# A hybrid encoder's second layer: the first attention units' buffers move, and two tiles' first key pairs come first

## The chip, the cores and the metric

The kernel runs on one core of a Trainium2 chip. The metric is the device time of one execution in microseconds (us): 3005.96 us is the median of three runs of the kernel before (3002.47, 3012.47, 3005.96). The engines are TensorE (PE; its weight loads are listed as PEld), VectorE (DVE), ScalarE (ACT), GpSimd (POOL) and SyncE (SP), which here only issues transfers.

## The reference

A two-layer encoder over 2048 tokens of width 1024, all in float32. Layer 0 (a state-space scan and a convolution branch) is not touched by the change. Layer 1 projects the normed input to q, z, k, v and to a small indexer; the indexer scores every admissible key, each query keeps its best 256 keys, and attends to these alone with 16 heads of 64 over 4 key/value heads:

```python
isc = jax.nn.relu(jnp.einsum("bqhd,bsd->bqhs", qib, ki))
score = jnp.einsum("bqh,bqhs->bqs", wib, isc)
score = jnp.where((key_chunk <= c)[None, None, :], score, -jnp.inf)
_, idx = lax.top_k(score, ksel)
...
logits = jnp.einsum("bqhgd,bqkhd->bqhgk", qb, kg) * scale
logits = jnp.where(valid[:, :, None, None, :], logits, -jnp.inf)
ob = jnp.einsum("bqhgk,bqkhd->bqhgd", softmax(logits), vg)
return (out * jax.nn.silu(z)) @ w_out      # then residual and a final RMSNorm
```

## The kernel before

Layer 1 has three stages, in `layer1` and `layer1_out`.

*Index and projections.* The 2048 rows go through in two halves of 1024 (`project_half`). A half's normed features lie in SBUF as eight blocks, hb0 to hb7, of 8 KB a partition, each split in a high and a low part; a product of two float32 matrices is three matmuls (`mm3`: high by high, high by low, low by high). The normed input comes through four buffers xt1 of 4 KB. Each group of 256 output columns has its weights loaded (wst), split (wh on ACT, wl on POOL) and multiplied; q, z, k, v and the indexer's parts go to DRAM. `index_scores` computes the indexer's scores; `select_mask` finds the 256th best by a binary search over sort keys made of the scores' bits (key, khi, klo on DVE and ACT; a step is a count, on DVE or as a Sign on ACT, and two steps on the small tile sv, on POOL or DVE) and writes a mask to DRAM. Tiles 0 to 11 of 16 (128 queries each) are done before the last projections. Tiles 12 to 15 are done by `late`, a generator whose next step is taken beside the projections (140 steps) and then beside the attention (every 800 columns): it loads a tile's scores (scr) from DRAM (sc_d) and runs `select_mask`.

*Attention.* A unit is a query tile i and a pair of key heads kp, two half-units (hp) each; the order of tiles is the table ORDER (3, 7, 4, 6, ...), and of a tile first kp 0, then kp 1. The keys lie in SBUF, high and low part, with the values, in four sets: kh00, kl00, v00 for keys 0 to 1023 and pair 0, kh01.. for pair 1, kh10.. and kh11.. for keys 1024 to 2047. A k part is 1024 KB, a v 512 KB. `Attend.load` brings a unit's mask (amb), queries (qt) and gate (zt_a); `stacks` splits the queries on POOL into tmq, transposes them on PE (ps_q), copies them on ACT (qs); `weights` multiplies with the keys (ps_s), adds the mask and takes the minimum on DVE (lm, mx, line 1099), and takes the exp on ACT (line 1110); `values` transposes (ps_pt), copies (pT), multiplies with the values (ps_pv, line 1133), transposes back (ps_ot) and gates (zr, avt, zt_a).

*Output.* `layer1_out` loads the output weights in two halves of columns (wst3), splits them into a high part (ACT, line 1334) and a low part (POOL, some on DVE), and then takes 16 tiles: transposes (ps_t), products (ps_o), norm, store. In the code wo00 and wo10 are the high and the low part of the first half, wo01 and wo11 of the second.

What sets the order: the code is run once by a tile framework, which builds a list of instructions with their dependences and then schedules each engine's queue by its own estimate of times; a tile's memory is waited for as a whole (`reuse_waits="tile"`). Memory comes from pools stacked from the left or the right end of a partition; a pool opened where an earlier one was closed lies on the same bytes, and its first write waits for the earlier tiles' last reads. All loads and stores go through SP's one queue.

## Time and profile before

| | |
|---|---|
| median of three runs | 3005.96 us (3002.47 to 3012.47) |
| the profiled execution | 3008.15 us, its span 3006.3 us |
| granted clock of TensorE, mean over the span | 0.969 |
| PE busy | 2754.0 us, 92% of the span |
| DVE, ACT, POOL busy | 2127.9, 1694.8, 1118.3 us |
| layer 1 begins / last product of the projections / attention ends | about 960 / 1804.7 / 2809 us |
| chain that ended last, by engine | PE 41%, DVE 19%, issue 6%, ACT 5%, POOL 5%, DMA 3% |

All times are of one profiled execution and counted from the beginning of its span. A granted clock of 1.00 is 2.4 GHz, 0.50 is 1.2 GHz. Where a row names what an engine waited for, it is the one that came last by the profile's semaphore events.

### The profile page before, as it was taken

The numbers are of one execution on the slowest core, as the hardware profiler recorded it, in microseconds if no ns is written. First come the engines' busy times: TensorE is split into PE (matmuls) and PEld (weight loads), VectorE is DVE, ScalarE is ACT, GpSimd is POOL, SyncE is SP. The second block draws the span as 40 slices with busy tenths as digits, with TensorE's granted clock in tenths as the row PEclk, the third lists the DMA queues.
The fourth block names the chain that finished last, engine by engine and source line by source line (L and its number), as shares of the span: only waits on it lengthen the run. The fifth ranks groups of instructions, "written<-read, shape, count | busy, mean of one in ns | idle before, by whom it ended". The sixth has DMA issues, their size and how long they took to land.

```text
span 3006.3 us, 47629 instructions
## 1 busy us (share of the span) xinstructions
PE 2754.0 (92%) x17488; PEld 2223.8 (74%) x17488; DVE 2127.9 (71%) x4121; ACT 1694.8 (56%) x3202; POOL 1118.3 (37%) x1453
## 2 busy tenths in 40 slices
PE   7779998799999999899789898999989999999998
PEld 5657786677999898888778885666655666666787
DVE  8889895996354478979997877876777444456444
ACT  4122333334243688778856558888887767655311
POOL 3946132642231587765665323322322101001000
PEclk9889899899999999999899998999999999999999
DMA  3263554356557323223432424110110101001332
GB/s 135 72 131 127 161 158 81 114 168 194 183 186 249 100 71 109 77 84 104 140 109 77 128 92 162 38 57 29 61 38 28 49 18 43 22 5 50 123 126 98
DMA packets 233385, 300.40 MB, mean 100 GB/s; under 512 B 14144, under 2 KB 171072, under 8 KB 233024
## 3 DMA queue, kind: packets, MB, share of 16 engines
q1 hardware_dynamic: 233152, 297.37, 31.5%
q8 instruction: 137, 2.24, 0.3%
q14 instruction: 96, 0.79, 0.1%
HBM read 194.16 MB, written 105.25 MB: 100 GB/s over the span
## 4 chain that ended last, share of the span: by engine, by line
PE 41%; DVE 19%; issue 6%; ACT 5%; POOL 5%; DMA 3%; SPq 0%; DVEq 0%; ACTq 0%; POOLq 0%
PE ps_pv L1133 9%; PE ps_pt L1126 8%; PE ps_s L1095 7%; DVE eq L976 6%; PE ps_tm L121 2%; PE ps_tm L122 2%; PE ps_tm L123 2%; PE ps_o L122 2%; PE ps_o L121 2%; PE ps_o L123 2%; DVE scl L72 2%; POOL sv L69 2%; ACT eq L986 1%; DVE cum L1026 1%; POOL wl L114 1%
## 5 line engine op out<-in xcount | busy, mean ns | idle before, releaser
L114 POOL TENSOR_TENSOR wl<-wst,wh 128x512 fp32r<-128x512 f32 (+1 forms) x220 | 339.0, 1544 | 389.6 <-ACT wh L113 377.8
L121 PE MATMUL ps_tm<-wh,hb 128*128 128x256 f32 (+1 forms) x1536 | 439.4, 290 | 11.7 <-ACT ot L875 7.5
L122 PE MATMUL ps_tm<-wh,hb 128*128 128x256 f32 (+1 forms) x1536 | 444.1, 290 | 0.2 <-DVE hb L72 0.2
L123 PE MATMUL ps_tm<-wl,hb 128*128 128x256 f32 (+1 forms) x1536 | 438.8, 289 | 0.0
L1099 DVE CUSTOM_DVE_ANT_0 lm<-ps_s,amb 128x1024 f32<-128x1024 f32 (+7 forms) x256 | 250.3, 987 | 200.1 <-PE ps_pt L1126 117.2
L72 DVE SCALAR_TENSOR_TENSOR cvo<-hc,vec,cvo 128x1024 f32<-128x1024 f32 x240 | 359.3, 1529 | 0.8
L1131 ACT COPY pT<-ps_pt 128x512 f32<-128x512 f32 (+1 forms) x512 | 273.9, 564 | 152.3 <-PE ps_pt L1126 130.1
L1133 PE MATMUL ps_pv<-pT,v 128*64 128x256 f32 x2176 | 339.3, 398 | 14.4 <-DVE avt L62 7.5
L1126 PEld LDWEIGHTS ps_pt<-ident,lm 128*128 128x128 f32 x2176 | 240.1, 141 | 145.4 <-issue 124.5
L1126 PE MATMUL ps_pt<-ident,lm 128*128 128x128 f32 x2176 | 339.1, 282 | 6.1 <-ACT pT L1131 4.0
L1110 ACT ACTIVATE lm<-lm,mx 128x512 f32<-128x512 f32 (+15 forms) x256 | 309.1, 1211 | 62.9 <-DVE mx L1099 62.4
L69 POOL TENSOR_SCALAR sv<-sv 128x1 f32<-128x1 f32 x448 | 185.5, 415 | 382.6 <-DVE eq L976 296.5
L121 PEld LDWEIGHTS ps_tm<-wh,hb 128*128 128x128 f32 x1536 | 296.2, 194 | 21.2 <-ACT ot L875 9.2
L122 PEld LDWEIGHTS ps_tm<-wh,hb 128*128 128x128 f32 x1536 | 297.7, 194 | 6.0 <-DVE hb L72 0.6
L123 PEld LDWEIGHTS ps_tm<-wl,hb 128*128 128x128 f32 x1536 | 296.4, 194 | 4.8
L113 ACT CAST wh<-wst 128x512 fp32r<-128x512 f32 (+1 forms) x220 | 133.4, 610 | 277.2 <-DMA wst<-in_w_in 122.3
L1095 PE MATMUL ps_s<-kh,qs 128*128 128x512 f32 (+2 forms) x640 | 264.9, 415 | 19.4 <-DVE mx L1099 17.9
L121 PE MATMUL ps_p<-hh,wh 128*128 128x512 f32 x640 | 258.5, 406 | 19.1 <-ACT uT L520 16.0
L123 PE MATMUL ps_p<-hl,wh 128*128 128x512 f32 x640 | 258.9, 407 | 0.0
L122 PE MATMUL ps_p<-hh,wl 128*128 128x512 f32 x640 | 257.5, 403 | 0.0
L1095 PE MATMUL ps_s<-kl,qs 128*128 128x512 f32 (+2 forms) x640 | 233.4, 370 | 0.0
L913 ACT ACTIVATE relu<-ps_i 128x512 f32<-128x512 f32 (+3 forms) x304 | 161.0, 545 | 104.5 <-DVE scl L72 55.3
(327 smaller groups left out, 6353.0 us busy)
## 6 DMA issues: line engine op xcount, KB each, us to landing
wst<-in_w_in SPq DMA_DIRECT2D x168, 256.0 KB, 2.9
zs_d<-zt SPq DMA_DIRECT2D x16, 512.0 KB, 3.5
zt<-zs_d SPq DMA_DIRECT2D x16, 512.0 KB, 4.5
ry<-rec_d SPq DMA_DIRECT2D x16, 512.0 KB, 4.2
xr<-in_x SPq DMA_DIRECT2D x16, 512.0 KB, 4.3
wst<-in_w_out SPq DMA_DIRECT2D x32, 256.0 KB, 3.3
h_d<-xr SPq DMA_DIRECT2D x16, 512.0 KB, 3.5
xt<-h_d SPq DMA_DIRECT2D x16, 512.0 KB, 6.1
```

The lines of the kernel that those rows point to most:

```text
L69: eng.tensor_scalar(out=out, in0=a, scalar1=s1, scalar2=s2, op0=op0, op1=op1)
L72: self.nc.vector.scalar_tensor_tensor(out=out, in0=a, scalar=s, in1=b, op0=op0, op1=op1)
L114: nc.gpsimd.tensor_tensor(out=lo, in0=st, in1=hi.bitcast(F32), op=ALU.subtract)
L121: t.matmul(ps, a[0], b[0], start=start, stop=False)
L122: t.matmul(ps, a[1], b[0], start=False, stop=False)
L123: t.matmul(ps, a[0], b[1], start=False, stop=stop)
L1095: nc.tensor.matmul(pss[e][:, cols], qs[e][:, 2 * hp + h], src[:, e, cols], start=part == 0, stop=part == 1)
L1099: self.pace[0] = nc.vector.tensor_tensor_reduce(out=prob[e][h][:, c:c + w], in0=pss[e][:, 0:w], in1=mb[:, c:c + w], scale=-0.125, scalar=( ...
L1110: nc.scalar.activation(lm, lm, AF.Exp, bias=mxs[e, h][:, nh - 1:nh], scale=-1.0, accum_out=t["den"][:, hd:hd + 1])
L1126: nc.tensor.transpose(ps[:, s, h], prob[e][h][:, (b + s) * P:(b + s + 1) * P], ident)
L1131: nc.scalar.copy(pT[:, 0:n], ps[:, 0:n].rearrange("p s h q -> p s (h q)"))
L1133: nc.tensor.matmul(po[64 * s:64 * s + 64, e], self.kvt[(b + s) // 8, kp][2][:, (b + s) % 8, e * 64:e * 64 + 64], pT[:, s], start=b == 0, s ...
```

## The change

It places buffers anew and changes two orders in the code. Places in bytes of a partition, before and after:

| tiles | before | after |
|---|---|---|
| hb0 to hb7 (projections) | 163808 to 229344 | 147424 to 212960 |
| xt1 | 147424 to 163808, four tiles of 4 KB | 212960 to 229344, two pairs of 8 KB; later kh00 and kl00 |
| kh00, kl00, v00 | 25600 to 46080 | in the pair tiles of xt1; v00 at 146848 (over hb0) |
| kh01, kl01, v01 | 46080 to 66560 | 25600 to 46080 |
| kh10 to v11 | 188384 to 229344 (over hb3 to hb7) | 48544 to 89504 (over the index stage) |
| qt / qs | 143328 / 69024 | 180192 (over hb4) / 196576 (over hb6, hb7) |
| pT, zt_a | 126944, 109984 | 150944, 159136 (over hb0 to hb2) |
| lm (two pools) | 155616 and 85408 | 114080 (over the weights) and 89504 |
| output weights, low part of the first half (wo10) | 27392 to 43776, over kh00, kl00, v00 | the same bytes, over kh01, kl01, v01 |

The code now loads kh00 and kl00 before the steps of `late`, v00 after the first unit's `load`, the second pair after that, and attends (3,0), (7,0), (3,1), (7,1) before going on as before. All instructions are as before in number and kind; new functions are `load_k` and `load_v`, in the diff.

```diff
--- before.py
+++ after.py
@@ -833,12 +833,11 @@
 
     for grp in range(4 if new else 0):
         with k.tc.high_priority(offset=1500):
-            tiles = []
-            for i in range(2):
-                xt = xp.tile([P, D], F32, tag="xt", name="xt1")
+            pair = xp.tile([P, 2, D], F32, tag="xt", name="xt1")
+            tiles = [pair[:, i] for i in range(2)]
+            for i, xt in enumerate(tiles):
                 r0 = h * HALF + (grp * 2 + i) * P
                 nc.sync.dma_start(xt, h1_d[r0:r0 + P])
-                tiles.append(xt)
             norm_to_feature(k, tiles, 1, hT, grp * 256, vec, ident, sm, ev, pt, parts=2)
 
     def finish(c, ot, t0):
@@ -1168,9 +1167,9 @@
         pool = lambda c, name, bufs, **kw: c.enter_context(
             tc.tile_pool(name=name, bufs=bufs, reuse_waits="tile", **kw))
 
+        xp = pool(ctx, "xp1", 2, side="right")
         with ExitStack() as c2:
             hp = pool(c2, "hp1", 1, side="right")
-            xp = pool(c2, "xp1", 4, side="right")
             pt = pool(c2, "pt1", 2, space=PSUM)
             tags = lambda **n: {t: pool(c2, t + "1", b, side="right") for t, b in n.items()}
             wp, ev, sm = tags(junk=1, wh=8, wst=2), {}, tags(ss=2, rs=2, rsqh=2, rsqt=2)
@@ -1236,22 +1235,25 @@
             tk = pool(ctx, "tk2", 1)
             kvt = {}
 
-            def open_kv(half, kp, kv_pool):
+            def open_kv(half, kp, kv_pool, v_pool=None):
                 n = f"{half}{kp}"
-                kvt[half, kp] = (kv_pool.tile([P, 2, HALF], F32R, name="kh" + n),
-                                 kv_pool.tile([P, 2, HALF], F32R, name="kl" + n),
-                                 kv_pool.tile([P, 8, 128], F32, name="v" + n))
-
-            def load_kv(half):
+                kw = {"tag": "xt"} if kv_pool is xp else {}
+                kvt[half, kp] = (kv_pool.tile([P, 2, HALF], F32R, name="kh" + n, **kw),
+                                 kv_pool.tile([P, 2, HALF], F32R, name="kl" + n, **kw),
+                                 None if v_pool is None else v_pool.tile([P, 8, 128], F32, name="v" + n))
+
+            def load_k(half, kp):
                 r = slice(half * HALF, half * HALF + HALF)
-                for kp in range(2):
-                    kh, kl, v = kvt[half, kp]
-                    nc.sync.dma_start(kh.bitcast(F32), S["kh"][2 * kp:2 * kp + 2, :, r].rearrange("v p n -> p v n"))
-                    nc.sync.dma_start(kl.bitcast(F32), S["kl"][2 * kp:2 * kp + 2, :, r].rearrange("v p n -> p v n"))
-                    nc.sync.dma_start(v, S["v"][r, kp * 128:kp * 128 + 128].rearrange("(t p) c -> p t c", p=P))
-
-            for kp in range(2):
-                open_kv(0, kp, pool(ctx, f"kva{kp}", 1))
+                for part in range(2):
+                    src = S[("kh", "kl")[part]][2 * kp:2 * kp + 2, :, r]
+                    nc.sync.dma_start(kvt[half, kp][part].bitcast(F32), src.rearrange("v p n -> p v n"))
+
+            def load_v(half, kp):
+                src = S["v"][half * HALF:half * HALF + HALF, kp * 128:kp * 128 + 128]
+                nc.sync.dma_start(kvt[half, kp][2], src.rearrange("(t p) c -> p t c", p=P))
+
+            kva = pool(ctx, "kva1", 1)
+            open_kv(0, 1, kva, kva)
 
             def late():
                 for j in range(LATE, 16):
@@ -1265,26 +1267,33 @@
             half(1, False, rest)
             swap_h(False)
             half(0, False, rest)
+            open_kv(0, 0, xp)
+            load_k(0, 0)
             for _ in range(EARLY):
                 next(beside)
-            load_kv(0)
         with ExitStack() as c3:
-            open_kv(1, 0, pool(c3, "kvb0", 1, side="right"))
-            open_kv(1, 1, pool(c3, "kvb1", 1, side="right"))
-            pp0 = pool(c3, "pp0", 4, side="right")
-            am, tm = pool(c3, "am", 1, side="right"), pool(c3, "tm", 1, side="right")
-            ptp, ap_ = pool(c3, "ptp", 4, side="right"), pool(c3, "ap", 1, side="right")
-            pp1, qsp = pool(c3, "pp1", 3, side="right"), pool(c3, "qsp", 1, side="right")
+            qsp, tm = pool(c3, "qsp", 1, side="right"), pool(c3, "tm", 1, side="right")
+            am, ap_ = pool(c3, "am", 1, side="right"), pool(c3, "ap", 1, side="right")
+            ptp = pool(c3, "ptp", 4, side="right")
+            v00 = pool(c3, "kva0", 1, side="right").tile([P, 8, 128], F32, name="v00")
+            kvt[0, 0] = (*kvt[0, 0][0:2], v00)
+            pp0, pp1 = pool(c3, "pp0", 4, side="right"), pool(c3, "pp1", 3, side="right")
+            for kp in range(2):
+                kvb = pool(c3, f"kvb{kp}", 1, side="right")
+                open_kv(1, kp, kvb, kvb)
             pools = (am, tm, qsp, ap_, (pp0, pp1), ptp, pool(c3, "pq", 2, space=PSUM),
                      pool(c3, "pt2", 3, space=PSUM), pool(c3, "pv", 1, space=PSUM))
             at = Attend(k, S, kvt, pools, ident, identr, beside, pace)
-            halves = [(i, kp) for i in ORDER for kp in range(2)]
+            a, b = ORDER[0:2]
+            halves = [(a, 0), (b, 0), (a, 1), (b, 1)] + [(i, kp) for i in ORDER[2:] for kp in range(2)]
             loaded = {}
 
             def load(n):
 
                 if n == SECOND:
-                    load_kv(1)
+                    for kp in range(2):
+                        load_k(1, kp)
+                        load_v(1, kp)
                 for i, kp in halves[n:n + 1]:
                     while i not in done:
                         next(beside, None)
@@ -1297,7 +1306,10 @@
 
             pend = None
             load(0)
+            load_v(0, 0)
             ready(0)
+            load_k(0, 1)
+            load_v(0, 1)
             for n in range(len(halves)):
                 for hp_ in range(2):
                     unit = (loaded[n], hp_, at.weights(loaded[n], hp_))
```

The names in the rows below end in a number that tells tiles of one name apart; scr, qt, z_d and so on are as above. SP's queue at the beginning of the attention, before:

```order
L931 DMA sc_d_7965<-scl_13389 128x512
L1250 DMA kl01_13457<-kl_d_7962 128x2x1024
L1251 DMA v01_13458<-v_d_7963 128x8x128
L860 DMA z_d_7958<-ot_18521 128x4x256
L1259 DMA scr_18828<-sc_d_7965 128x1792
L1033 DMA mask_d_7964<-eq_18685 128x1664
L1054 DMA amb_18929<-mask_d_7964 128x512
L1058 DMA qt_18931<-q_d_7957 128x512
```

and in the changed kernel:

```order
L930 DMA sc_d_7965<-scl_13381 128x512
L859 DMA z_d_7958<-ot_18507 128x4x256
L1249 DMA kl11_18905<-kl_d_7962 128x2x1024
L1253 DMA v11_18906<-v_d_7963 128x8x128
L1249 DMA kh10_18898<-kh_d_7961 128x2x1024
L1249 DMA kl10_18899<-kl_d_7962 128x2x1024
L1253 DMA v10_18900<-v_d_7963 128x8x128
L1261 DMA scr_18818<-sc_d_7965 128x1792
L1053 DMA amb_18916<-mask_d_7964 128x512
L859 DMA z_d_7958<-ot_18613 128x4x256
L1032 DMA mask_d_7964<-eq_18675 128x1664
L1057 DMA qt_18918<-q_d_7957 128x512
```

kl11, v11, kh10, kl10 and v10 stand in place of kl01 and v01 between the score store and scr, and the last z_d (ot_18613) and mask_d stand ahead of the first qt.

DVE's queue at the first score tiles (the ISA rows are the score tile's pass and its read-out of mx, line 1099, now 1098), before:

```order
L69 TENSOR_SCALAR key_18850<-scr_18828 128x256
L62 TENSOR_TENSOR key_18850<-key_18850,scr_18828 128x256
L970 COPY khi_18831<-key_18850 128x256
L1099 ISA lm_18961,mx_18962<-ps_s_18965,amb_18929 128x512
L1099 ISA mx_18962 128x1
L1099 ISA lm_18963,mx_18964<-ps_s_18966,amb_18929 128x512
L1099 ISA mx_18964 128x1
L69 TENSOR_SCALAR sv_18833<-sv_18833 128x1
L72 SCALAR_TENSOR_TENSOR sv_18833<-sv_18833 128x1
L976 TENSOR_SCALAR eq_18830,sv_18833<-khi_18831,sv_18833 128x1792
```

and in the changed kernel:

```order
L69 TENSOR_SCALAR key_18840<-scr_18818 128x256
L62 TENSOR_TENSOR key_18840<-key_18840,scr_18818 128x256
L969 COPY khi_18821<-key_18840 128x256
L69 TENSOR_SCALAR sv_18823<-sv_18823 128x1
L72 SCALAR_TENSOR_TENSOR sv_18823<-sv_18823 128x1
L975 TENSOR_SCALAR eq_18820,sv_18823<-khi_18821,sv_18823 128x1792
L1098 ISA lm_18954,mx_18955<-ps_s_18958,amb_18916 128x512
L1098 ISA mx_18955 128x1
L1098 ISA lm_18956,mx_18957<-ps_s_18959,amb_18916 128x512
L1098 ISA mx_18957 128x1
L69 TENSOR_SCALAR sv_18823<-sv_18823 128x1
```

The two sv steps and the first count over khi now stand ahead of the first score tile and no longer behind it; on ACT a second Sign stands ahead of the first exp.

POOL's queue at the end of the attention (wo10 and wo11: low parts of the output weights; zt_a of tile 15 last), before:

```order
L62 TENSOR_TENSOR zt_a_27084<-zt_a_27084,avt_28350 128x2x128
L62 TENSOR_TENSOR wo10_29010<-wst3_29011,wo00_29009 128x1024
L62 TENSOR_TENSOR wo10_29010<-wst3_29015,wo00_29009 128x1024
L62 TENSOR_TENSOR zr_28788<-zt_a_27526,rd_28786 128x256
L62 TENSOR_TENSOR wo10_29010<-wst3_29019,wo00_29009 128x1024
L62 TENSOR_TENSOR zt_a_27084<-zt_a_27084,avt_28570 128x2x128
L62 TENSOR_TENSOR wo10_29010<-wst3_29023,wo00_29009 128x1024
L62 TENSOR_TENSOR zr_28948<-zt_a_27526,rd_28946 128x256
L62 TENSOR_TENSOR zt_a_27526<-zt_a_27526,avt_28791 128x2x128
L62 TENSOR_TENSOR wo11_29046<-wst3_29051,wo01_29045 128x1024
L62 TENSOR_TENSOR zt_a_27526<-zt_a_27526,avt_28951 128x2x128
L62 TENSOR_TENSOR wo11_29046<-wst3_29059,wo01_29045 128x1024
```

and in the changed kernel:

```order
L62 TENSOR_TENSOR zt_a_27075<-zt_a_27075,avt_28561 128x2x128
L62 TENSOR_TENSOR zr_28939<-zt_a_27517,rd_28937 128x256
L62 TENSOR_TENSOR zt_a_27517<-zt_a_27517,avt_28782 128x2x128
L62 TENSOR_TENSOR wo10_29002<-wst3_29003,wo00_29001 128x1024
L62 TENSOR_TENSOR wo10_29002<-wst3_29007,wo00_29001 128x1024
L62 TENSOR_TENSOR zt_a_27517<-zt_a_27517,avt_28942 128x2x128
L62 TENSOR_TENSOR wo10_29002<-wst3_29011,wo00_29001 128x1024
L62 TENSOR_TENSOR wo10_29002<-wst3_29015,wo00_29001 128x1024
L62 TENSOR_TENSOR wo11_29038<-wst3_29043,wo01_29037 128x1024
L62 TENSOR_TENSOR wo11_29038<-wst3_29051,wo01_29037 128x1024
```

The four wo10 rows stood among the last units' zr and zt_a rows, and now stand behind all but one of them.

## Rows read from the trace of the kernel before

**Rows 1.** Windows: us, busy PE, PEld, DVE, ACT, POOL; clock, DMA share, GB/s.
```profile
960.00:1804.70 844.70, 760.81 (x5512) 712.67 (x5511) 671.65 (x1370) 596.84 (x1274) 511.00 (x778) 0.97 0.32 100
1804.70:2809.00 1004.30, 954.36 (x6185) 635.99 (x6184) 631.12 (x1309) 738.77 (x1271) 206.42 (x352) 0.99 0.14 46
```

**Rows 2.** Chain of waits, attention's beginning: start us, us, what.
```profile
1802.23 5.45 DMA scr<-sc_d
1807.70 0.44 DVE key L69
...
1819.19 1.52 ACT lm L1110 x4
```

**Rows 3.** Timeline of SP's issues there: start us, us, line, operation, out<-in.
```profile
1793.39 0.33 SPq L931 DMA_DIRECT2D sc_d<-scl  x1
1793.82 0.39 SPq L1250 DMA_DIRECT2D kl<-kl_d  x1
1794.30 0.46 SPq L1251 DMA_DIRECT2D v<-v_d  x1
...
1802.23 0.33 SPq L1259 DMA_DIRECT2D scr<-sc_d  x1
...
1804.00 0.48 SPq L1058 DMA_DIRECT2D qt<-q_d  x1
```

**Rows 4.** Timeline of POOL there; in square brackets idle time, releaser.
```profile
1809.90 1.20 POOL L769 CAST tmq<-qt 128x256 fp32r<-128x256 f32 x2 [21.14 <-DMA qt<-q_d]
...
1820.47 0.64 POOL L69 TENSOR_SCALAR sv<-sv 128x1 f32<-128x1 f32 x2 [4.66 <-DVE eq L976]
```

**Rows 5.** Timeline of PE, same stretch.
```profile
1812.01 1.62 PE L772 MATMUL ps_q<-identr,tmq 128*128 128x128 f32 x8 [7.28 <-POOL tmq L770]
```

**Rows 6.** Windows at the seam, columns as in the first group.
```profile
1795.00:1803.00 8.00, 8.00 (x69) 8.00 (x68) 7.72 (x4) 0.74 (x2) 0.00 (x0) 1.00 0.90 260
...
1811.00:1817.00 6.00, 3.93 (x13) 2.67 (x14) 5.46 (x10) 3.50 (x6) 4.61 (x7) 0.50 1.05 409
1829.00:1875.00 46.00, 42.06 (x260) 28.03 (x259) 38.02 (x79) 44.69 (x83) 15.44 (x33) 1.00 0.17 57
```

**Rows 7.** Timeline of DVE at the first score tile.
```profile
1809.54 0.43 DVE L69 TENSOR_SCALAR key<-scr 128x512 int32<-128x512 int32 x1 [0.22 <-ACT klo L971]
...
1815.25 0.70 DVE L970 COPY khi<-key 128x256 uint16<-128x256 uint16 x1
...
1818.29 2.08 DVE L976 TENSOR_SCALAR_CACHE_REDUCE eq<-khi,sv 128x1792 bf16<-128x1792 uint16 x1
```

**Rows 8.** Timeline of ACT at the first exp.
```profile
1815.99 1.79 ACT L986 ACTIVATE eq<-khi,sv 128x1792 bf16<-128x1792 uint16 x1 [0.33 <-DVE khi L970]
1817.69 0.19 ACT L986 ACTIVATION_READ_ACCUMULATOR eq<-khi,sv 128x1 f32 x1
1817.89 1.28 ACT L1110 ACT_TABLE_LOAD   x1
```

**Rows 9.** Timeline of PE at the end of the attention.
```profile
2806.97 1.52 PE L1133 MATMUL ps_pv<-pT,v 128*64 128x256 f32 x12
2809.17 0.66 PE L1141 MATMUL ps_ot<-ident,ov 128*128 128x128 f32 x4 [0.69 <-ACT ov L1137]
2810.38 0.66 PE L1349 MATMUL ps_t<-ident,xa 128*128 128x128 f32 x4 [0.56 <-DVE yl L62]
...
2812.04 0.40 PE L123 MATMUL ps_o<-wo,yh 128*128 128x512 f32 x1
2812.28 0.39 PE L121 MATMUL ps_o<-wo,yh 128*128 128x512 f32 x1
```

**Rows 10.** Timeline of POOL in the last units of the attention.
```profile
2768.41 2.40 POOL L62 TENSOR_TENSOR wo<-wst,wo 128x1024 fp32r<-128x1024 f32 x1 [1.47 <-ACT wo L1334]
...
2811.07 0.74 POOL L62 TENSOR_TENSOR zt_a<-zt_a,avt 128x256 f32<-128x256 f32 x1 [2.25 <-DVE avt L62]
```

**Rows 11.** DMA issues, 1780 to 1830: KB each, median us to landing.
```profile
sc_d<-scl SPq DMA_DIRECT2D x1, 256.0 KB, 2.3
```

## The prediction

> **What bounds the kernel now.** I read first the busy times by stage [rows 1]. In the attention, from the last product of the projections at 1804.7 us to about 2809, TensorE is busy for 954.36 of 1004.30 us; in the layer-1 stretch before it, 760.81 of 844.70. So the attention can get shorter by some 50 us at most, and whatever moves its beginning or its end as a whole moves the kernel's end with it. The change touches the seam at each side: the loads that lie ahead of the first attention unit, and the memory that the output projection's weights wait for.
>
> Then the chain of waits at the first seam [rows 2]. It runs neither through the projections nor through the keys of the attention, but through the selection of tile 12 to 15 that goes on beside: DVE ends a selection, SP issues the next tile's scores (scr) at 1802.23, they are read at 1807.70, DVE and ACT make sort keys of them, and only then comes the first score tile and, at 1819.19, the first exp. SP's issues [rows 3] show scr as one piece of a queue: one queue carries everything, and the load of scr stands behind kl01 and v01. The first qt, issued at 1804.00, is what POOL waits for until 1809.90 [rows 4], and TensorE stands idle for 7.28 us behind POOL [rows 5]. From 1829 on ACT is busy for 44.69 of 46 us [rows 6], so the beginning of the attention is bound by ACT: nothing there gives a late start back.
>
> **The change, part by part.** (1) *Start: the queue.* Once a score store (sc_d) has gone out at 1793.39 after a long wait, SP now issues kl11, v11, one z_d, kh10, kl10 and v10 ahead of scr, where kl01, v01 and the z_d stood [rows 3]. A k part is 1024 KB (1.05 MB), a v 512 KB: 4.98 MB with sc_d instead of 2.36, so 2.62 MB more. These landed in order of issue in the trace. The rate is the unknown: 1795 to 1803 moved 260 GB/s at a share of 0.90, with just such loads and a store; 1811 to 1817, with k and v loads alone, 409 [rows 6]. From 1793.8, 4.98 MB take 12.2 us at 409 (1806.0) and 19.2 us at 260 (1813.0). scr is 0.92 MB, 2.2 or 3.5 us more: DVE can begin at 1808.2 to 1816.5 instead of 1807.70. I take the middle, 1812.4, 4.7 us later; neither row is nearer, as the new queue is k and v loads like the one, with stores and the projections beside it like the other. The first qt comes behind scr, amb, the last z_d and mask_d (1.08 MB more), and with its own 0.26 MB lands 3.3 to 5.2 us after scr, at 1811.5 to 1821.7; from qt's use to the first exp it is 9.3 us now (1809.90 to 1819.19) [rows 2, 4], so by that path exp comes at 1821 to 1831. The path through scr is a little longer:
>
> (2) *Start: the order on DVE and ACT.* Between the last key copy and the first score tile there now stand a Sign on ACT, two small sv steps, a 128x1792 count on DVE, the sv steps on POOL, and a second Sign on ACT ahead of the first exp. Key steps: 8.25 us from 1807.70 until the last copy ends at 1815.95 [rows 2, 7]; the first 512 of 1792 columns took 1.84 us (1807.70 to 1809.54), and 3.5 times that is 6.4, so 6.4 to 8.25. With the big loads now ahead of them and not beside them I take 7.3. Then Sign 1.9 (1815.99 to 1817.88), sv 0.4 (to 1818.29), count 2.1, POOL's sv 0.8 with its start, second Sign 1.9, table load 1.3 [rows 4, 7, 8]: 15.7 us from scr to exp, at 1828.1, 8.9 us later than 1819.19. Of that the second Sign is work only pulled forward (it ran behind the first exps before): 1.9 less. **Start: +7.0 us**; bounds: 1808.2 + 14.8 - 1819.19 - 1.9 = +1.9, and 1816.5 + 16.6 - 1819.19 - 1.9 = +12.0.
>
> (3) *End.* The low parts of the first half of the output weights are laid over 27392 to 43776 bytes of a partition. There lay kh00, kl00 and v00, out of use when the last tile's first key pair was done; now there lie kh01, kl01 and v01, read until the last value product, which ends at 2808.49 [rows 9]. So four POOL subtractions of 2.40, all of them now through by 2771 in the middle of the last tiles, come behind that end, with one zt_a step of 0.74 between [rows 10]: 10.3 us until the last is done. TensorE has the transposes of ps_ot (0.66) and 18 of the first tile's 24 products at one in 0.24 us (2812.04, 2812.28), 4.2 us, to do meanwhile [rows 9]: 5.4 us idle, instead of 0.69 + 0.56 now [rows 9]. **End: +4 us**. Bounds: 0, if other products fill the gap, and +10, if none do.
>
> (4) *The rest.* The pair tile for two xt, the early loads of kh00 and kl00, the order (3,0), (7,0), (3,1), (7,1): the instructions are the same ones, and no engine waits for a load after the first qt in this part of the trace; 0. The scheduler also shifts instructions in the projections and the index stage, with no row that says in which direction: 0, with 5 us to either side, a tenth of the 50 us that TensorE stands idle in the attention [rows 1].
>
> Sum: +11 against the profiled execution's 3008.15 us, 3019; that execution is 2.2 us above the median of the runs shown, so **3017 us**.
>
> **Rivals.** *A. The loads drain in time.* If the queue runs at 409 GB/s already before 1804, scr is read 0.5 us later; the start costs +1.9, the end's gap is filled, and the kernel is at about 3008. For: the loads are issued while TensorE still has 10 us of products, and the higher rate is in the trace. Against: with the same neighbours it was 260. In the Trainium skill, "DMA: Bandwidth & Descriptors", section "Rules for kernel authors", the advice is to issue a load early and to wait for it late; by that alone the start would cost nothing and the sum would be the end's +4, some 3010. No row of before shows the loads early enough to tell.
>
> *B. A clean start.* This ends faster. At the seam the clock is 0.50 from 1811 to 1817 and the DMA share 1.05 [rows 6], while the key steps take 8.25 instead of 6.4 us. If all k and v loads are done before scr is issued at 1802.23, scr is read some 3.0 us sooner (2.3 us after its issue, as the 256 KB of sc_d [rows 11], at 1804.6), the key steps take 1.8 less, and TensorE, idle for less, may keep its full clock: half of some 9 us of products, 4.5. Together 9.3 less, 2999 against the profiled execution, 2997 against the median, with the end hidden. It decides at the rate: 4.98 MB in 8.4 us are 590 GB/s, and the fastest of the rows has 409. Against it too: the two Signs and the count now stand ahead of the first exp.
>
> *C. The change does not do what it says.* qt now lies where feature block 4 of the projections lay, which is read until the last few products, so "free sooner" may hold of names alone; if the first units begin as they did, and only the end's cost is left, 3008.15 + 4 - 2.2 = 3010.
>
> **How the numbers follow.** A measurement of this kernel tells some 0.3%, 9 us, from no change: over 3015 is slower, under 2997 faster. The forecast (start late, end exposed) has 0.50; A 0.26; C 0.12; B 0.07; 0.05 is left for shifts in the middle, to either side. Slower: most of the forecast and little else, 0.50. Same: A, C and the low part of the forecast, 0.40. Faster: B and part of the rest, 0.10. The range takes A and C in below, down to start +1.9, end 0 and middle -5 (3003), and above start +12.0 with end +4 less 2.2 and some of the middle: 3002 to 3028.
>
> **What would show it.** In the profile of the changed kernel: scr issued near 1802 but read only near 1812; the first qt landing after 1814; the first exp near 1828; TensorE's idle time ahead of its first ps_q 10 us or more instead of 7.28; at the end an idle of some 5 us in front of a ps_o product, released by POOL's wo. Wrong would be: scr read before 1809, a first exp before 1822, no idle behind POOL's wo, or a difference that arises before 1790, in the projections.

## The result and the profile after

The changed kernel takes 3026.61 us, the median of six runs (3017.12 to 3036.65), the kernel before in the same comparison 3003.91 us (six runs, 2999.80 to 3012.47). The ratio is 1.0067 with a 95% interval of 1.0044 to 1.0091: slower by some 20 us, with both ends of the interval above 9 us. The time lies inside the range that was given, the direction is the one forecast, and the size is not: +11 us had been forecast. Of all executions reported here one was slow, 5131.85 us among the twelve of e7, and the figures of e7 are those of the other eleven.

The profiled execution of the changed kernel spans 3025.8 us, 19.5 more than that of before. The engines' work is the same, as the first lines of its page show:

```profile
span 3025.8 us, 47605 instructions
...
PE 2757.8 (91%) x17488; PEld 2226.5 (74%) x17488; DVE 2118.9 (70%) x4121; ACT 1695.4 (56%) x3202; POOL 1125.6 (37%) x1453
```

PE is busy for 3.8 us more and every instruction count is as before, so the loss is mostly waiting, and at the end some slower clock. To find where, I compare the two traces at points which both kernels pass in the same order. The rows zr on POOL are one per half-unit of the attention, 64 in all; the 62nd stands in the last tile. Before:

```profile
2738.35 0.61 POOL L62 TENSOR_TENSOR zr<-zt_a,rd 128x256 f32<-128x256 f32 x1 [23.05 <-DVE rd L1144]
```

and after:

```profile
2749.88 0.61 POOL L62 TENSOR_TENSOR zr<-zt_a,rd 128x256 f32<-128x256 f32 x1 [23.05 <-DVE rd L1143]
```

By the profiles' own clocks 11.53 us of the 19.5 are lost by then. The two executions do not start layer 1 at the same time, though. The first store of q (a row of SP's queue) comes in the kernel before at

```profile
1195.40 0.37 SPq L860 DMA_DIRECT2D q_d<-ot  x1
```

and in the changed one at

```profile
1193.31 0.37 SPq L859 DMA_DIRECT2D q_d<-ot  x1
```

Counted from there the 62nd zr row is 13.6 us later in the changed kernel: scr is issued 2.0 us later (606.8 and 608.8 us after that store), and the other 11.7 us lie between scr's issue and the last tile. How much of the 2.0 us is the change's is open, since the runs below scatter: 607.0 to 607.7 in e1, e10 and e11, edits of the kernel before, and 607.4 to 608.7 in e3 to e6 and e12, edits of the changed one. Towards the very end nothing more is lost: in the last 126.8 us before the last copy of a transposed output tile (yh on ACT), TensorE does the same 582 matmuls without a gap, before

```profile
2860.00:2986.78 126.78, 126.78 (x582) 101.60 (x581) 59.58 (x172) 24.86 (x63) 0.00 (x0) 1.00 0.35 121
```

and after (columns as in [rows 1])

```profile
2879.45:3006.24 126.79, 126.79 (x582) 101.69 (x581) 59.55 (x172) 24.84 (x62) 0.00 (x0) 1.00 0.35 121
```

so the other 8 us are lost between the last tile of the attention and the first tiles of the output. From the 62nd zr row to that last yh row it was 248.43 us and is 256.36; for the same 1280 matmuls TensorE is busy 5.6 us longer and idle 2.3 us longer:

```profile
2738.35:2986.78 248.43, 247.19 (x1280) 187.52 (x1279) 122.01 (x305) 73.62 (x139) 19.30 (x13) 1.00 0.34 115
```

```profile
2749.88:3006.24 256.36, 252.78 (x1280) 188.69 (x1279) 120.70 (x305) 74.11 (x138) 18.92 (x13) 0.99 0.32 107
```

**The start.** The chain of waits after, at the place of [rows 2]:

```profile
1802.10 7.53 DMA scr<-sc_d
1809.65 0.44 DVE key L69
...
1817.04 1.89 ACT eq L985 x2
...
1824.09 1.28 ACT L1109
1825.38 0.82 ACT lm L1109 x2
```

scr is read 7.55 us after its issue, not 5.47; the first exp starts at 1825.38, not 1819.19. SP's queue at the place of [rows 3]:

```profile
1790.12 0.33 SPq L930 DMA_DIRECT2D sc_d<-scl  x1
...
1794.32 0.54 SPq L1253 DMA_DIRECT2D v<-v_d  x1
1802.10 0.33 SPq L1261 DMA_DIRECT2D scr<-sc_d  x1
...
1804.54 0.90 SPq L1057 DMA_DIRECT2D qt<-q_d  x1
```

The score store went out 3.3 us sooner than in [rows 3] (1.2 us counted from the first store of q), and the five loads behind it from 1791.03 to 1794.32; scr and the queries stand behind these, and landed late. On DVE the first count stands ahead of the first score tile,

```profile
1818.95 0.15 DVE L69 TENSOR_SCALAR sv<-sv 128x1 f32<-128x1 f32 x1 [1.95 <-ACT eq L985]
...
1819.34 2.08 DVE L975 TENSOR_SCALAR_CACHE_REDUCE eq<-khi,sv 128x1792 bf16<-128x1792 uint16 x1
...
1821.34 0.69 DVE L1098 CUSTOM_DVE_ANT_0 lm<-ps_s,amb 128x512 f32<-128x512 f32 x1
```

and on ACT two Signs stand ahead of the first exp, the second behind POOL:

```profile
1817.04 1.79 ACT L985 ACTIVATE eq<-khi,sv 128x1792 bf16<-128x1792 uint16 x1
...
1822.19 1.79 ACT L985 ACTIVATE eq<-khi,sv 128x1792 bf16<-128x1792 uint16 x1 [2.31 <-POOL sv L69]
...
1825.38 0.72 ACT L1109 ACTIVATE lm<-lm,mx 128x512 f32<-128x512 f32 x1
```

TensorE had its last product of the projections at 1796.73, 5.6 us sooner than before when counted from the first store of q (603.4 us after it, not 609.1), and got nothing for it: the idle time in front of the first ps_q grew from 7.28 us [rows 5] to

```profile
1815.25 1.62 PE L772 MATMUL ps_q<-identr,tmq 128*128 128x128 f32 x8 [18.24 <-POOL tmq L770]
```

**The end.** POOL's subtractions for the low weights (wo) now wait for a value product of the last unit, and the last of these products (PE) ends at 2818.03:

```profile
2814.18 4.69 POOL L62 TENSOR_TENSOR wo<-wst,wo 128x1024 fp32r<-128x1024 f32 x2 [12.28 <-PE ps_pv L1132]
...
2821.70 4.68 POOL L62 TENSOR_TENSOR wo<-wst,wo 128x1024 fp32r<-128x1024 f32 x2
```

```profile
2816.95 1.08 PE L1132 MATMUL ps_pv<-pT,v 128*64 128x256 f32 x8
```

TensorE waits for them twice, ACT waits for the weights of the second half, which are loaded through the same two buffers, and the granted clock falls (PE, then ACT, then a window):

```profile
2824.10 0.50 PE L123 MATMUL ps_o<-wo,yh 128*128 128x512 f32 x1 [2.05 <-POOL wo L62]
...
2826.43 0.80 PE L123 MATMUL ps_o<-wo,yh 128*128 128x512 f32 x1 [0.54 <-POOL wo L62]
```

```profile
2827.68 1.04 ACT L1346 CAST wo<-wst 128x1024 fp32r<-128x1024 f32 x1 [3.87 <-DMA wst<-in_w_out]
```

```profile
2825.00:2833.00 8.00, 7.19 (x19) 4.82 (x18) 1.83 (x2) 2.72 (x4) 3.14 (x2) 0.57 0.62 195
```

### The profile page after: what moved, and what is told of

It reads as the page before. It is cut to its first block, busy times and chain, and to the rows that moved or that the text cites. A ratio compares the mean times of both kernels' runs of the same rounds, so it can differ in the third digit from the quotient of the medians.

```text
span 3025.8 us, 47605 instructions
## 1 busy us (share of the span) xinstructions
PE 2757.8 (91%) x17488; PEld 2226.5 (74%) x17488; DVE 2118.9 (70%) x4121; ACT 1695.4 (56%) x3202; POOL 1125.6 (37%) x1453
## 4 chain that ended last, share of the span: by engine, by line
PE 41%; DVE 18%; issue 6%; POOL 6%; ACT 5%; DMA 3%; SPq 0%; DVEq 0%; ACTq 0%; POOLq 0%
PE ps_pv L1132 9%; PE ps_pt L1125 8%; PE ps_s L1094 7%; DVE eq L975 6%; PE ps_tm L121 2%; PE ps_tm L122 2%; PE ps_tm L123 2%; PE ps_o L122 2%; PE ps_o L121 2%; PE ps_o L123 2%; POOL sv L69 2%; DVE scl L72 2%; ACT eq L985 1%; POOL wl L114 1%; DVE lm L1098 1%
## 5 line engine op out<-in xcount | busy, mean ns | idle before, releaser
L1109 ACT ACTIVATE lm<-lm,mx 128x1024 f32<-128x1024 f32 (+15 forms) x256 | 308.9, 1210 | 67.4 <-DVE mx L1098 66.9
L1094 PE MATMUL ps_s<-kh,qs 128*128 128x512 f32 (+2 forms) x640 | 265.8, 417 | 21.5 <-DVE mx L1098 18.8
L1132 PEld LDWEIGHTS ps_pv<-pT,v 128*64 128x64 f32 x2176 | 131.6, 136 | 117.2 <-issue 52.0
```

The costliest lines, as they stand in the source:

```text
L1094: nc.tensor.matmul(pss[e][:, cols], qs[e][:, 2 * hp + h], src[:, e, cols], start=part == 0, stop=part == 1)
L1109: nc.scalar.activation(lm, lm, AF.Exp, bias=mxs[e, h][:, nh - 1:nh], scale=-1.0, accum_out=t["den"][:, hd:hd + 1])
L1132: nc.tensor.matmul(po[64 * s:64 * s + 64, e], self.kvt[(b + s) // 8, kp][2][:, (b + s) % 8, e * 64:e * 64 + 64], pT[:, s], start=b == 0, s ...
```

## The experiments

All changes are small edits of one of the two kernels. Since the time at which layer 1 reaches its first store of q differs between profiled executions (1191.6 to 1200.6 us), the table reads each profile from its own rows; every figure of a stretch is a difference of two rows of the same profile. For the two kernels in which scr no longer comes ahead of the first queries, the first two columns are empty. Each ratio is to executions of the kernel before in the same comparison (their medians lie between 3003.9 and 3007.3 us). A profile is one execution: up to the 62nd zr row, the kernel before, e1 and e11, whose starts have the same order, lie 3.3 us apart from scr's issue and 3.5 us from the first store of q, so differences of that size say nothing.

| kernel | scr's issue to first exp | scr's issue to 62nd zr | first exp to 62nd zr | first store of q to 62nd zr | 62nd zr to last yh | median, ratio to before (interval) |
|---|---|---|---|---|---|---|
| before | 16.96 | 936.1 | 919.2 | 1543.0 | 248.4 | 3003.9 |
| changed | 23.28 | 947.8 | 924.5 | 1556.6 | 256.4 | 3026.6, 1.0067 (1.0044 to 1.0091) |
| e1 before, end exposed | 16.11 | 937.0 | 920.9 | 1544.7 | 257.7 | 3017.5, 1.0034 (1.0020 to 1.0048) |
| e2 changed, end undone | 27.18 | 952.0 | 924.8 | 1554.7 | 249.1 | 3020.8, 1.0053 (1.0038 to 1.0069) |
| e3 changed, old pair order | 23.28 | 949.2 | 925.9 | 1556.6 | 254.2 | 3025.4, 1.0065 (1.0041 to 1.0088) |
| e4 changed, loads behind qt | 21.89 | 941.8 | 919.9 | 1549.2 | 254.5 | 3021.5, 1.0061 (1.0045 to 1.0077) |
| e5 changed, 124 steps | 19.34 | 927.2 | 907.8 | 1535.9 | 254.2 | 3012.2, 1.0009 (0.9995 to 1.0023) |
| e6 changed, 124 steps, loads behind qt | 17.43 | 929.7 | 912.2 | 1537.8 | 255.9 | 3011.8, 1.0010 (0.9996 to 1.0023) |
| e7 changed, end undone, queries first | | | 933.1 | 1544.1 | 249.1 | 3015.8, 1.0020 (1.0009 to 1.0031) |
| e8 before, 110 steps | | | 935.9 | 1549.3 | 248.4 | 3014.6, 1.0021 (1.0008 to 1.0035) |
| e9 changed, end undone, 124 steps | 24.66 | 935.2 | 910.5 | 1537.5 | 249.1 | 3002.1, 0.9991 (0.9982 to 1.0001) |
| e10 before, 124 steps | 17.01 | 926.8 | 909.8 | 1534.5 | 248.4 | 2995.9, 0.9961 (0.9946 to 0.9976) |
| e11 before, pair tile | 17.18 | 939.4 | 922.3 | 1546.5 | 248.4 | 3004.8, 0.9994 (0.9983 to 1.0005) |
| e12 changed, count's place | 19.32 | 939.8 | 920.4 | 1547.6 | 254.5 | 3021.2, 1.0056 (1.0035 to 1.0077) |

The first theory: the start and the end cost separately, the start by the loads ahead of scr and by the order of pairs, the end by the memory under the weights. Its rivals: the schedule as a whole, or, at the start, the order on DVE and ACT.

**e1: the end alone.** In the kernel before, the two sets kva0 and kva1 change places:

```diff
-            for kp in range(2):
+            for kp in (1, 0):
                 open_kv(0, kp, pool(ctx, f"kva{kp}", 1))
```

> The kernel before, with the two first-half key sets exchanged on the left stack: kh01, kl01, v01 now lie where the low part of the first output weights goes, and nothing at the attention's start is moved. Theory (the two seams cost separately): the first exp and the step to the last tile stand as in the kernel before, and the end alone grows by about 8 us, as in the changed kernel (the last PE rows shift by 19.45 us there, 11.5 of them before the last tile): some 3012 us. Rival (the end is late only because of the shifted schedule before it): no change, 3004 us.

Measured 3017.5 us; the ratio gives 10 us (6 to 14) where 8 had been expected. From scr's issue to the 62nd zr row nothing moves beyond 1 us, and the rest takes 257.7 instead of 248.4. TensorE's waits at the end of that kernel (timeline of PE), and the clock behind them (window):

```profile
2818.38 0.50 PE L123 MATMUL ps_o<-wo,yh 128*128 128x512 f32 x1 [1.88 <-POOL wo L62]
...
2822.49 0.80 PE L121 MATMUL ps_o<-wo,yh 128*128 128x512 f32 x1 [2.91 <-ACT wo L1334]
...
2824.92 0.80 PE L123 MATMUL ps_o<-wo,yh 128*128 128x512 f32 x1 [1.21 <-POOL wo L62]
```

```profile
2819.00:2833.00 14.00, 9.89 (x34) 7.13 (x33) 2.55 (x3) 4.81 (x6) 4.74 (x2) 0.76 0.60 212
```

So the memory under the weights alone makes the end's cost, in the kernel before too.

**e2: the changed kernel without it.** The first pair lies on the left stack and the second in the pair tiles (all five places, of which two are shown):

```diff
-            open_kv(0, 1, kva, kva)
+            open_kv(0, 0, kva, kva)
...
-            open_kv(0, 0, xp)
-            load_k(0, 0)
+            open_kv(0, 1, xp)
+            load_k(0, 1)
```

> The changed kernel, with the first key pair in the left stack and the second one in the pair tiles, so that the output weights' low part lies over the first pair's tiles again, which are free early. Theory: the start stays as late as in the changed kernel (first exp near 1825), the end's 8 us are gone: some 3018 us, idle before ps_o under 1.5 us. Rival: the time stays near 3026, because the weights' loads, two buffers deep, are what is late and not the memory under them.

The end is back at 249.1 us, and the only waits of TensorE from 2780 to 2870 are

```profile
PE ps_ot L1140 <- ACT ov L1136: 0.7, 1, 0.7
PE ps_o L121 <- ACT wo L1346: 0.3, 1, 0.3
```

The timed median is 5.9 us below that of the changed kernel, and the two intervals overlap, so the size is taken from the profile. At the start, scr was issued at 1798.44, 6.1 us earlier than in the changed kernel (both counted from the first store of q), and was read only 2.5 us earlier, 11.1 us after its issue:

```profile
1809.57 0.43 DVE L69 TENSOR_SCALAR key<-scr 128x512 int32<-128x512 int32 x1 [10.53 <-DMA scr<-sc_d]
```

That is the queue: the last of the loads ahead of scr landed at 1807.2, and scr was read 2.4 us after it; in the changed kernel these are 1807.5 and 2.2 us. It is also why 952.0 us from scr's issue look worse than the changed kernel's 947.8: from the first store of q the 62nd zr row comes 1.9 us earlier.

**e3: the pairs' order.**

```diff
-            halves = [(a, 0), (b, 0), (a, 1), (b, 1)] + [(i, kp) for i in ORDER[2:] for kp in range(2)]
+            halves = [(i, kp) for i in ORDER for kp in range(2)]
```

> The changed kernel with the tiles' key pairs in the old order: (3,0), (3,1), (7,0), (7,1). Theory (3.5 of the start's 9.75 us come from the pairs' order, as TensorE waits for copies and DVE for the selection's Signs inside the first two tiles): the first exp stays near 1825, the steady shift after the first two tiles falls from 9.75 to about 6: some 3022 us. Rival (they come from the late start and the half clock whatever the order): no change, 3026 us.

The theory fell: from scr's issue to the 62nd zr row it is 949.2 us, 1.4 more than in the changed kernel. The new order of pairs neither costs nor gains anything that these runs tell.

**e4: the loads.** The six loads get an edge to the first load of queries on SP's queue:

```diff
-                    nc.sync.dma_start(kvt[half, kp][part].bitcast(F32), src.rearrange("v p n -> p v n"))
+                    op = nc.sync.dma_start(kvt[half, kp][part].bitcast(F32), src.rearrange("v p n -> p v n"))
+                    if half:
+                        k.after(op, at.q0)
```

(the same for v; at.q0 is the first dma of qt).

> The changed kernel with the six loads of the second half's keys and values issued behind the first unit's queries (an order on SP's queue, nothing else). Theory A (the queue costs): scr is read near 1805 instead of 1809.65, the first exp comes near 1820 instead of 1825.4, the steady shift falls from 9.75 to about 5: some 3021 us. Theory B (the order on DVE and ACT costs, with two Signs and a count ahead of the first exp, and the loads then run beside the key steps): first exp 1823 or later, no change beyond 2 us.

scr is read 5.6 us after its issue, as theory A has it, and the run to the 62nd zr row is 6.0 us shorter. But the first exp still comes 21.89 us after scr's issue, 4.9 more than in the kernel before: theory B was right for that part. Each theory explains one half. The timed runs do not show the 6.0 us by themselves (3021.5 us, 1.0061 against 1.0067), and the profiled execution, 3017.3 us, was the lowest of the nine.

**e5, e6: the order, with and without the loads.** With fewer early steps of the selection, the first count is no longer among them, and falls behind the first score tiles.

```diff
-EARLY = 140
+EARLY = 124
```

> The changed kernel with 124 instead of 140 early steps of the selection, so that on DVE the first count over khi stands behind the first score tiles again and on ACT one Sign, not two, ahead of the first exp; the six loads still stand ahead of scr. From scr's issue to the first exp it was 16.96 us in the kernel before, 23.28 in the changed one, 21.89 with the loads behind. Theory (the order is most of it, about 5 us; the loads 1.4): 18 to 19.5 us from scr's issue to the first exp, bounded then by the first queries' landing. Rival (loads and order overlap, either alone is enough): still 22 us or more.

> The changed kernel with 124 early steps and the six loads issued behind the first queries. Theory (order and loads are all of the start's loss): 16.5 to 17.5 us from scr's issue to the first exp as in the kernel before, and from scr's issue to the 41st zr row no more than 2 us over the kernel before; only the end's 8 us are left: some 3012 us. Rival (the pairs' order or the new places cost on their own): 5 us or more over the kernel before at the 41st zr row.

Both came out as the theory has it for the first exp (19.34 and 17.43 us), and much further on than expected: to the 62nd zr row 927.2 and 929.7 us, less than the kernel before's 936.1. So the 124 steps did two things at once, and two further runs had to tell them apart (e10, e12). With them, the loads' place makes no difference that these runs tell (2.5 us the wrong way round in the profiles, 3012.2 and 3011.8 us timed).

**e7, e8: the queries first.** Fewer steps still (110), so that scr's load is not ahead of the queries; in e7 with the edits of e2 and e4.

> The changed kernel without the end's cost (first pair on the left stack), with the six loads behind the first queries, and with 110 early steps, so that neither the load of scr nor the wait for the selection stands ahead of the first queries on SP. Theory (what bounds the attention's start in both kernels is scr, on SP ahead of the queries, and the selection on DVE): the first exp comes within 15 us of the last projection product and the time falls to 2995 to 3000 us, below the kernel before. Rival (the selection's steps only move into the attention and are paid there, as ACT is busy for 97% of its first stretch): 3004 us or more.

> The kernel before with 110 instead of 140 early steps, nothing else: the first queries are issued ahead of scr. Theory as for the run on the changed kernel with the queries first: the first exp some 6 to 9 us earlier, the time 2995 to 2999 us. Rival (paid inside the attention): no change, 3004 us.

The theory fell in both; they take 3015.8 and 3014.6 us, some 6 us more than the kernel before by their ratios, and more than the rival's 3004. In e7 the first exp starts at 1804.53, 12.7 us sooner than in the kernel before when counted from the first store of q, and the 62nd zr row comes no sooner (1.2 us later):

```profile
1804.53 0.72 ACT L1110 ACTIVATE lm<-lm,mx 128x512 f32<-128x512 f32 x1
```

```profile
2737.59 0.61 POOL L62 TENSOR_TENSOR zr<-zt_a,rd 128x256 f32<-128x256 f32 x1 [23.11 <-DVE rd L1144]
```

The start is paid inside the attention: from the first exp to that row it takes 933.1 us, 13.9 more than before. Here, starting sooner without having done the selection's steps is worth nothing.

**e9: both seams mended in the changed kernel**, the edits of e2 and e5 together.

> The changed kernel without the end's cost (first pair on the left stack) and with 124 early steps (count behind the first score tiles). From the profiles so far: with 124 steps the run from scr's issue to the 41st zr row was 527.9 us (534.3 in the kernel before, 545.9 in the changed one), the stretch after it 2.5 us shorter, and with the end undone the rest 249 instead of 256 us. Theory (the pieces add): 2996 to 3002 us, under the kernel before. Rival (with the end undone scr is issued some 3 us sooner behind the same loads, which land no sooner): 3004 us or more.

3002.1 us, 0.9991 of before with an interval across 1. That is no proof that all of the change's loss is back, for the 124 steps also make the kernel before faster (e10, next). Against that one, timed in the same comparison, e9 is 6.2 us slower, and the intervals of the two ratios do not overlap: a part of the loss is left. Where it lies the profiles do not tell: the end takes 0.7 us longer, and the 62nd zr row comes 3.1 us later from the first store of q, which is within their scatter. scr went out at 1797.73 and was read 11.3 us later, so part of the rival is right: the loads set when it lands. Whether they make what is left was not tried (the loads behind the queries on top of these two edits).

**e10: the 124 steps in the kernel before**, nothing else.

> The kernel before with 124 early steps, nothing else. Theory (the 124 steps help wherever the selection and the first tiles share ACT and DVE, whatever the places of the buffers): from scr's issue to the 41st zr row 526 to 530 us instead of 534.3, the time 2996 to 3001 us. Rival (the gain in the changed kernel was only the return of what the order had lost): no change, 3004 us.

2995.9 us, 0.9961 of before (0.9946 to 0.9976): the fastest of all kernels here (the kernel before had 3005.5 us in that comparison). Its first exp starts at the same place as before's, its 62nd zr row 9.2 us earlier (9.3 from scr's issue):

```profile
1819.38 0.72 ACT L1110 ACTIVATE lm<-lm,mx 128x512 f32<-128x512 f32 x1
```

```profile
2729.18 0.61 POOL L62 TENSOR_TENSOR zr<-zt_a,rd 128x256 f32<-128x256 f32 x1 [23.05 <-DVE rd L1144]
```

The number of early steps is thus worth 9 us by itself, apart from the change, and of the three numbers tried the middle one is best, as 110 steps cost 6 us (e8). Which of the moved steps brings it was not tried.

**e11: the pair tile alone**, in the kernel before.

```diff
-                xt = xp.tile([P, D], F32, tag="xt", name="xt1")
+            pair = xp.tile([P, 2, D], F32, tag="xt", name="xt1")
...
-            xp = pool(c2, "xp1", 4, side="right")
+            xp = pool(c2, "xp1", 2, side="right")
```

> The kernel before with the two normed inputs of a group in one pair tile (two of 8 KB instead of four of 4 KB), nothing else. In the changed kernel the projections' last product comes some 8 us sooner after the first query store than in the kernel before (about 596 instead of 604 us). Theory (the pair tile alone reorders the projections and brings this, and it is lost again because the selection's scr bounds the start): the last product near 596 us after the first query store, the first exp no sooner after scr's issue than 16 us, the time within 3 us of the kernel before. Rival (the 8 us come from the new places of hb or of the keys): the last product stays near 604 us after the first query store.

The theory fell: the last product came 609.3 us after the first query store, as in the kernel before (609.1), not 603.4 as in the changed one (596 and 604 in the expectation are both too low). The pair tile costs nothing and does not bring the shorter projections; which of the other places does stays open.

**e12: the count's place alone.** The changed kernel with all 140 steps, and one edge on DVE:

```diff
         if pace and pace[0]:
             k.after(op, pace[0])
+        elif pace and i == LATE + 1:
+            pace.append(op)
...
+                    while len(self.pace) > 1:
+                        k.after(self.pace.pop(), self.pace[0])
                     self.cols += 2 * w
```

> The changed kernel with all its 140 early steps and its loads ahead of scr; one order is added: the first count over khi stands behind the first score tile on DVE (so that one Sign, not two, is ahead of the first exp). From scr's issue to the 62nd zr row it was 936.1 us in the kernel before, 947.8 in the changed one, 927.2 in the changed one with 124 steps, 926.8 in the one before with 124 steps. Theory (the count's place is the change's loss at the start, the number of steps a gain of 9 us of its own that both kernels could have): about 936 us there, the end's 8 us left, some 3012 us. Rival (the number of steps is all of it, the count's place nothing): 944 us or more, 3022 us.

In the profile the first exp comes 19.32 us after scr's issue, as with 124 steps, and the 62nd zr row 939.8 us after it: 8.0 less than in the changed kernel, 3.6 more than in the one before, between the theory's 936 and the rival's 944. On DVE:

```profile
1818.31 0.69 DVE L1100 CUSTOM_DVE_ANT_0 lm<-ps_s,amb 128x512 f32<-128x512 f32 x1 [1.40 <-PE ps_s L1096]
...
1818.92 2.07 DVE L975 TENSOR_SCALAR_CACHE_REDUCE eq<-khi,sv 128x1792 bf16<-128x1792 uint16 x1
```

The timed runs (3021.2 us, 1.0035 to 1.0077) are what the rival had, not the theory's 3012, and do not tell this kernel from the changed one; the profiled execution, 3015.4 us, was the lowest of the six. So that the count's place is most of the start's loss is read from one profile of each kernel and is not shown in the time. That the number of steps is a matter of its own is shown by e10.

## Why the prediction was right in sign and short in size

*What bounds.* Right: the start hangs on scr and the selection, not on the projections. The projections' last product came 5.6 us sooner than in the kernel before (from the first store of q), which I had costed at 0 with 5 us to either side, and the time did not notice. That is a difference in the projections, before 1790, which I had named as a sign of being wrong; it stopped at the wait for scr.

*Step 1, the queue.* Right in kind, within its bounds: scr was read at 1809.65, forecast 1812.4 (1808.2 to 1816.5). The loads went out earlier than I assumed, at 1791 to 1794, and the rate lay between my two rows: from the first of them to scr's reading 350 GB/s were moved (window, columns as in [rows 1]):

```profile
1791.00:1809.65 18.65, 6.01 (x51) 5.81 (x49) 11.42 (x13) 1.42 (x4) 0.00 (x0) 0.78 1.04 350
```

The first queries were used at 1813.14, inside 1811.5 to 1821.7.

*Step 2, the order.* Right: from scr's reading to the first exp 15.73 us, forecast 15.7. The key steps took 7.4 (1809.65 to 1817.0; forecast 7.3).

*The start's sum, "+7.0 us".* This is the first step that failed. The first exp came 6.3 us late from scr's issue (8.3 from the first store of q), no more than the 8.9 forecast, and I took 1.9 off because the second Sign was "work only pulled forward". Nothing of this came back. From the first exp to the 62nd zr row the changed kernel took 5.3 us more on top, for which the sum had no term. The start is +11.7 us from scr's issue, at the upper bound of +12.0, and +13.6 from the first store of q. By e4 the loads are 6.0 of the 11.7, by e12 the count's place 8.0, more than the whole together, so they are no separate parts. What adds the 5.3 us behind the first exp stays open: moving the loads takes 4.6 of it back (e4), and so does moving the count, 4.1 (e12), so neither makes it alone.

*The end, "+4 us".* The mechanism was right (e1, e2), the size half of what it is: 7.9 us, and 9.2 in e1, under the bound of +10. The four subtractions did not all come behind the last value product: the first two began at 2814.18, released by an earlier one, and the last was done 8.4 us after the last value product had ended at 2818.03, not 10.3. TensorE's idle time behind the attention is 3.2 us where 5.4 had been forecast, 1.9 more than before. Two things were not in the sum. The granted clock fell to 0.57 for 8 us, in which 7.19 busy us lost some 3.1 by that (an estimate, 0.43 of them). And the second half's weights, loaded through the two buffers that the late subtractions hold, came late: ACT waited 3.87 us for one of them. Of the 5.6 us by which the same matmuls are busy longer, some 2.5 are not placed by this.

*The rest, "0".* The pair tile (e11) and the pairs' order (e3) indeed cost nothing.

*The rivals.* A (the loads drain in time) did not come: scr was read 7.55 us after issue. B (a clean start) neither, for the reason given, the rate: it needed 590 GB/s. C (only the end's cost) neither, as the first exp did come later. The Trainium skill's advice in "DMA: Bandwidth & Descriptors", "Rules for kernel authors", is to issue early and wait late. By that alone the start would have cost nothing. e2 and e9 show a limit on one queue: the loads were early by more than 200 us for their own use (tile 8, the first to use them, is the sixth in the order), and scr, wanted at once, was read 11.1 and 11.3 us after its issue. With the loads behind the queries (e4) it was 5.6.

With the sizes measured, the sum is 13.6 + 7.9 = +21.5 from the first store of q, against 21.6 between the ends of the two profiled executions counted from there. The 19.5 us between their spans are less by the 2.1 us by which the changed kernel's execution was ahead at that store; that they nearly equal 11.7 + 7.9 is chance.

## What to carry to other kernels

A buffer moved to memory that is free sooner lets its load go out sooner, and on a queue shared with urgent loads that is no gift: ask what stands behind it, and whether the end of that chain was waiting for the load at all. A place that one tile leaves is taken by another; look up what is laid over the new place later, here the output weights over values that the last unit still reads. And where a scheduler sets the order, a change of places moves instructions on in-order engines: one 2 us count ahead of the first score tile cost no less than all the moved loads, by one profile each, and a number beside the change, how many steps of the selection are done early, was worth 9 us in the kernel before. So compare a mended kernel with the kernel before under the same setting, or the setting's gain passes for the repair's.

## What the runs showed of the hardware

Short waits of TensorE were followed by a lower granted clock. At the end of the changed kernel it waited 2.05, 0.54 and 0.27 us within 7 us, and the granted clock was 0.57 on average from 2825 to 2833, near the lower of its two levels, 0.50; by the estimate above that lost some 3.1 us, as much again as the 2.9 us of waits. In e1 it was 0.76 from 2819 to 2833, behind a wait of 1.88 us and with two more, of 2.91 and 1.21 us, inside: some 2.4 us lost (an estimate, 0.24 of 9.89 busy us) beside 6.0 us of waits. In the kernel before, with 0.69 and 0.56 us [rows 9], and in e2, with 0.69 and 0.29 us, it stayed at 1.00 there.
